# An output projection moved to Strassen's seven products, and two feed-forward prologues given other buffers and four PSUM banks

## The chip, the cores and the metric

The kernel runs on one core of a Trainium2 chip. It is one program; its time is the device time of one execution in microseconds (us). TensorE (PE in the profile) multiplies, VectorE (DVE), ScalarE (ACT) and GpSimd (POOL) work on tiles of 128 partitions, and SyncE (SP) issues the DMAs. Each engine takes its own instructions in order and waits for the others by semaphores.

## The reference, cut to what matters

One layer of a streaming encoder over 1024 tokens of width 1024, in float32:

```
x = x + 1/2 * SwiGLU_1(RMSNorm(x))          # FFN 1, inner width 2816
h = RMSNorm(x); P = h @ W_in
A = sparse attention of parts of P ;  M = mLSTM of other parts of P
x = x + W_out( sigmoid(g_a) * (A @ W_a) + sigmoid(g_b) * (M @ W_b) )
x = x + 1/2 * SwiGLU_2(RMSNorm(x))          # FFN 2
SwiGLU(h) = (silu(h @ w_gate) * (h @ w_up)) @ w_down
```

The change concerns the line with `W_out` (1024 x 1024), and the first step of both FFNs: RMSNorm, the transposes of the normed tokens, and the operands made of them.

## The kernel before, in words

**Precision.** Every float32 operand of a product is split in two: `hi` is a ScalarE copy rounded to the matmul's type, `lo` the VectorE (or GpSimd) difference. `mm3` (L658 to L660) then does three matmuls, hi·hi, hi·lo and lo·hi, of 128x128 by 128x512 each. `split` (L790 on ScalarE, L791 on VectorE) makes such a pair.

**Strassen's form.** The FFN products and the input projection use Winograd's form of Strassen's algorithm: both operands are cut in four blocks, sums and differences of blocks are made, and seven block products (numbered 0 to 6) stand for eight. `Presums` makes the sums of `W_in` once, beside the gate and up products of FFN 1 (`beside`), and stores them in DRAM (`d_s`).

**Prologue of an FFN** (`operands`). Four token tiles are normed (`norm`: Square with a sum on ScalarE L763, the root on VectorE L664 and GpSimd L665, the scaling on VectorE L765) into four buffers `xn` out of the arena `ar`. The squares of `norm` lie in a 1024 column buffer of the same arena. `turned` (L773) transposes 128 columns of four tiles into one of two PSUM banks (`psB`, banks 2 and 3), and `put_turned` evicts it twice on ScalarE (L841, L844) and once on VectorE (L842). After eight of these the four `xn` are freed, and tiles 4 to 7 are normed in place, transposed (evicted by L878) and combined (L879, L880, `put`, `put2`). `gate_up` starts with products 0 and 1 of two column blocks (96 matmuls), which need the first four tiles alone; product 5 needs the others.

**Memory.** `Segment`s are fixed stretches of SBUF in pages of 1024 columns. `ar` and `rr` are arenas over several of them, for plain and for split tiles; they hand out the space that was freed longest ago. `segment(tag, arena)` makes a stretch anew and so waits for its old users. In the first prologue `ar` has 11 pages: 4 `xn`, 4 results of L844, 2 of early weights, and what is left.

**Output projection** (`merge`). For each of eight column blocks c: load the gate (`d_sa`) and the other branch (`d_tb`), take the sigmoid (L2090), multiply `A @ W_a` (24 matmuls, `proj`), on VectorE times the gate and plus the branch (L2095, L2096), and split. After every second block `accumulate` multiplies the two finished blocks with two rows of `W_out` for all eight token tiles (96 matmuls, L805 to L809) and adds each 128x1024 result from PSUM onto the residual `xs` (L810). The rows of `W_out` come through `Weights`, which loads and splits ahead (L185 on ScalarE, L186 on GpSimd). `Pairs` (L240, L251 and L279 to L298) prepares the gate and up weights of FFN 2; its first operands are made before the last `accumulate`.

**Order.** A scheduler writes each engine's order by a simulated timeline, with program order as the priority; so later work can stand before earlier work where its operands come sooner.

`Down` (77 steps of 12 matmuls) is the last product of an FFN; each step splits an activation and a weight tile, loaded six steps ahead (L462).

Of the kernel before, what the change touches and what calls it, by code (L numbers as in the profile page):

```python
# [221 lines left out]
class Pairs:  # L222
# [82 lines left out]
    def prime(self):  # L305
        while self.nl < len(self.loads) and self._load():
            pass
        while self.np < min(len(self.jobs), self.i + self.LOOK) and self._prep():
            pass
# [9 lines left out]
class Presums:  # L319
# [6 lines left out]
    def __init__(self, k, w_in, d_s):  # L326
        self.k, self.w_in, self.d_s = k, w_in, d_s
        self.order = list(dict.fromkeys(i[0] for i in MIXING if i != "ik"))
        self.work = self.steps()

    def steps(self):
        k, nc = self.k, self.k.nc
        for p in self.order:
            two = [None, None]
            while not all(two):
                two = [k.ar.alloc(1024, soft=True) for _ in range(2)]
                if not all(two):
                    for b in two:
                        if b:
                            b.free()  # L340
                    yield
# [21 lines left out]

    def finish(self):
        left = sum(1 for _ in self.work)
        assert not left, left

# [61 lines left out]
class Down:  # L429
# [125 lines left out]
    def run(self, done):  # L555
        k = self.k
        for i, (q, j) in enumerate(self.steps):
            self.prime(i)
# [19 lines left out]
class Block:  # L578
    def __init__(self, tc, pools, a):
        self.tc, self.nc, self.a = tc, tc.nc, a  # L580
        self.sb, self.ps, self.dr = pools
        self.ar, self.rr, self.own = Arena(), Arena(), {}
        self.plain("plain", "more")
        self.round("round", "spare", "extra")
        for t in ("raw", "rawx", "side"):
            self.segment(t, None)
        self.whole_raw = True
        self.w = Weights(self, 0, 0)
        self.bg = ()
        self.due = [0, 0]  # L590

        self.psum = self.ps.tile([P, 4096], F32, name="psum", bufs=1)
        self.turn, self.turnB, self.turnS = 0, 2, 4
        self.last = None
# [26 lines left out]
    def segment(self, tag, arena):  # L621
# [8 lines left out]
        if arena:  # L630
            arena.segs.append(self.own[tag])

# [95 lines left out]
    def plan_weights(self):  # L728
# [8 lines left out]
        def rows(src, r0):  # L737
            v = src[r0:r0 + P, :]
            w.add(src.shape[1], lambda t: dma(t, v))

# [11 lines left out]
        for j in range(8):  # L752
            cols(a["w_proj_a"][0], j * P)
            if j % 2:
                rows(a["w_out"][0], (j - 1) * P)
                rows(a["w_out"][0], j * P)
# [12 lines left out]
    def turned(self, xn, k):  # L769

        ps = self.psB()
# [20 lines left out]


    def accumulate(self, xs, acts, ws, scale, done=None):

        nc = self.nc
        mm = nc.tensor.matmul
        last = len(acts) - 1
        for t in range(8):
            ps = self.psS()  # L800
            for j, (ac, w) in enumerate(zip(acts, ws)):
                ah, al = (b.r[:, t * P:(t + 1) * P] for b in ac)
                wh, wl = w[0].r, w[1].r
                for n in (0, 512):
                    mm(ps[:, n:n + 512], ah, wh[:, n:n + 512], start=j == 0, stop=False)  # L805
                for n in (0, 512):
                    mm(ps[:, n:n + 512], ah, wl[:, n:n + 512], start=False, stop=False)  # L807
                for n in (0, 512):
                    mm(ps[:, n:n + 512], al, wh[:, n:n + 512], start=False, stop=j == last)  # L809
            nc.vector.scalar_tensor_tensor(xs[t].f, ps, scale, xs[t].f, ALU.mult, ALU.add)  # L810
            if done:
                done(t)
        for pair in list(acts) + list(ws):
            for b in pair:
                b.free()
# [30 lines left out]
    def operands(self, xs, gain, spill=None):  # L846
# [6 lines left out]
        for t in range(4):  # L853
            n = ar.alloc(1024)
# [12 lines left out]
        yield 1  # L867
        for t in range(4, 8):
# [152 lines left out]
    def ffn(self, xs, gain, pairs, wd, x_dram, spill=None, first=None, done=None, beside=None):  # L1021
# [24 lines left out]
        down.run(done)  # L1046
# [3 lines left out]
    def late_tokens(self, xs, spill):  # L1050

        nc, v, gain = self.nc, self.nc.vector, self.g_mix
# [1026 lines left out]
    def merge(self, yaT, xs, next_pairs):  # L2079

        nc, ar = self.nc, self.ar
        acts = []
        for c in range(8):
            w = self.w.get()
            hi, lo = (self.either(1024, "side", "extra") for _ in range(2))
            sa, tb, sg = ar.alloc(1024), ar.alloc(1024), self.take("h0", 1024, False)
            nc.sync.dma_start(sa.f, self.d_sa[c])
            nc.sync.dma_start(tb.f, self.d_tb[c])
            with self.tc.issue_after(self.split_A):
                nc.scalar.activation(sg.f, sa.f, AF.Sigmoid)  # L2090
            for th in (1, 0):
                cs = slice(th * 512, th * 512 + 512)
                ps = self.psA(th)
                self.proj(w, yaT, th, ps)
                nc.vector.tensor_tensor(sg.f[:, cs], sg.f[:, cs], ps, ALU.mult)  # L2095
                nc.vector.tensor_tensor(sg.f[:, cs], sg.f[:, cs], tb.f[:, cs], ALU.add)  # L2096
                self.split(hi.r[:, cs], lo.r[:, cs], sg.f[:, cs])
            for b in (*w, sa, tb, sg):
                b.free()
            acts.append((hi, lo))  # L2100
            if c % 2:
                ws = [self.w.get(), self.w.get()]
                if c == 7:
                    self.close("more")
                    next_pairs.prime()
                self.accumulate(xs, acts, ws, 1.0)
                acts = []
        for pair in self.aqT.values():
            for b in pair:
                b.free()  # L2110


    def run(self, x, out):
# [28 lines left out]
        sums = Presums(self, a["w_in"][0], d_s)  # L2142
# [16 lines left out]
        self.ffn(xs, self.g_ffn1, pairs, a["ffn1_w_down"][0], xt, first=self.more_constants, done=half_done, beside=sums.step)  # L2159
# [71 lines left out]
        pairs = Pairs(self, a["ffn2_w_gate"][0], a["ffn2_w_up"][0])  # L2231
        self.merge(yaT, xs, pairs)
        self.segment("side", None)
        self.segment("h0", None)
        self.segment("swap", None)
        self.plain("more")
        self.round("extra")
# [47 lines left out]
```

## Time and profile before

| | us |
|---|---|
| median of 3 runs (2158.54 to 2163.19) | 2161.04 |
| the profiled execution | 2156.2 |
| its span, from the first to the last instruction | 2154.5 |
| TensorE busy in the span | 2067.5 (96%) |
| VectorE busy | 1632.2 (76%) |
| ScalarE busy | 1040.8 (48%) |
| granted TensorE clock, mean of the span | 0.988 |

A busy share is an average over stages with different limits, so the stages below are read one by one from windows of the span. A matmul's row gives its whole passage through the array (some 390 ns); what counts is the distance from one to the next, and that is read from how many fit in a window without a gap.

### The profile page before, as it was taken

Reading aid. Unit: us, or ns where it says so; the run is one execution under the profiler, and the core shown is the slowest. Engines: PE = TensorE matmul, PEld = TensorE weight load, DVE = VectorE, ACT = ScalarE, POOL = GpSimd, SP = SyncE. Lnnn points to the kernel's source line nnn. Section 1 sums busy time; section 2 is a strip of 40 time slices with the busy share of each in tenths; the row PEclk is TensorE's granted clock in tenths of the full one; section 3 lists DMA queues with packets and bytes.
Section 4 is the critical chain, followed back from the end, with each engine's and each line's share of the span. In section 5 each row is a group of like instructions: output and inputs, shape, how many; then the busy total and the mean of one; then the engine's idle time right before and its main releaser. Section 6 shows DMA issues by size and latency. Waiting matters only on the chain.

```text
span 2154.5 us, 27729 instructions
## 1 busy us (share of the span) xinstructions
PE 2067.5 (96%) x9397; PEld 1686.8 (78%) x9397; DVE 1632.2 (76%) x2806; ACT 1040.8 (48%) x1928; POOL 381.2 (18%) x391
## 2 busy tenths in 40 slices
PE   6999999999999999999998999899899999999999
PEld 5788787888887778677777787777688888888887
DVE  6987887678855885988899689665786667669964
ACT  7332233344446664965885578323633333334442
POOL 1000000000303224434445545221000000000300
PEclk9999999999999999999999999999899999999999
DMA  5379994393522324456775222612243333277341
GB/s 181 124 245 291 280 289 153 132 364 125 168 68 92 90 72 120 133 167 178 226 224 164 93 74 70 249 59 88 68 143 108 105 101 113 98 258 276 96 142 40
DMA packets 275466, 326.76 MB, mean 152 GB/s; under 512 B 20236, under 2 KB 185724, under 8 KB 275324
## 3 DMA queue, kind: packets, MB, share of 16 engines
q1 hardware_dynamic: 275324, 324.99, 46.5%
q8 instruction: 74, 1.21, 0.2%
q14 instruction: 68, 0.56, 0.1%
HBM read 224.23 MB, written 100.70 MB: 151 GB/s over the span
## 4 chain that ended last, share of the span: by engine, by line
PE 45%; DVE 10%; ACT 3%; DMA 2%; issue 2%; POOL 0%; SPq 0%; DVEq 0%; ACTq 0%; POOLq 0%
PE psum L658 12%; PE psum L660 12%; PE psum L659 12%; PE psum L1983 1%; DVE plain L1476 1%; PE psum L805 1%; PE psum L809 1%; PE psum L807 1%; DVE h L791 1%; PE psum L1365 1%; PE psum L2038 1%; PE psum L2037 1%; PE psum L1366 1%; ACT plain L1502 0%; ACT round L408 0%
## 5 line engine op out<-in xcount | busy, mean ns | idle before, releaser
L658 PE MATMUL psum<-h,round 128*128 128x512 f32 x656 | 261.8, 400 | 4.2 <-DVE plain L976 1.6
L659 PE MATMUL psum<-h,round 128*128 128x512 f32 x656 | 259.5, 396 | 1.1 <-DVE h L791 0.8
L660 PE MATMUL psum<-h,round 128*128 128x512 f32 x656 | 259.1, 395 | 0.3 <-DVE round L298 0.3
L545 POOL TENSOR_TENSOR swap<-swap,h 128x1024 f32<-128x1024 f32 x12 | 32.9, 2773 | 1014.8 <-DVE h L531 1014.8
L409 POOL TENSOR_TENSOR round<-raw,round 128x512 fp32r<-128x512 f32 x108 | 149.4, 1392 | 155.7 <-ACT round L408 122.1
L658 PEld LDWEIGHTS psum<-h,round 128*128 128x128 f32 x656 | 124.3, 190 | 33.9 <-DVE plain L976 2.0
L660 PEld LDWEIGHTS psum<-h,round 128*128 128x128 f32 x656 | 123.9, 189 | 27.9 <-issue 1.8
L659 PEld LDWEIGHTS psum<-h,round 128*128 128x128 f32 x656 | 124.2, 189 | 26.9 <-DVE h L791 1.3
L658 PE MATMUL psum<-swap,round 128*128 128x512 f32 x328 | 131.6, 406 | 9.9 <-ACT plain L1452 2.6
L660 PE MATMUL psum<-swap,round 128*128 128x512 f32 x328 | 129.9, 397 | 1.2 <-POOL round L409 1.2
L659 PE MATMUL psum<-swap,round 128*128 128x512 f32 x328 | 130.5, 398 | 0.1
L1476 DVE TENSOR_SCALAR_CACHE_REDUCE plain<-plain 128x384 bf16<-128x384 f32 (+1 forms) x124 | 100.3, 808 | 2.5
L297 ACT ACTIVATE round<-plain 128x512 fp32r<-128x512 f32 x75 | 46.8, 630 | 102.4 <-PE psum L659 80.6
L790 ACT ACTIVATE round<-plain 128x512 fp32r<-128x512 f32 x72 | 45.1, 631 | 102.2 <-PE psum L659 90.2
L658 PE MATMUL psum<-h,extra 128*128 128x512 f32 x200 | 80.2, 402 | 6.2 <-ACT h L790 4.9
L658 PEld LDWEIGHTS psum<-swap,round 128*128 128x128 f32 x328 | 63.2, 193 | 27.4 <-ACT plain L1452 3.0
L791 DVE TENSOR_TENSOR round<-plain,round 128x512 fp32r<-128x512 f32 x72 | 55.9, 780 | 37.6 <-ACT round L790 37.3
L408 ACT ACTIVATE round<-raw 128x512 fp32r<-128x512 f32 x108 | 66.4, 622 | 33.4 <-PE psum L659 20.6
L659 PE MATMUL psum<-h,extra 128*128 128x512 f32 x200 | 79.5, 397 | 2.2 <-DVE h L791 2.2
L658 PE MATMUL psum<-h,spare 128*128 128x512 f32 x200 | 78.8, 395 | 1.3 <-DVE plain L976 1.3
L660 PE MATMUL psum<-h,extra 128*128 128x512 f32 x200 | 79.0, 395 | 0.0
L659 PE MATMUL psum<-h,spare 128*128 128x512 f32 x200 | 78.4, 392 | 0.0
(753 smaller groups left out, 5972.5 us busy)
## 6 DMA issues: line engine op xcount, KB each, us to landing
plain<-d_a SPq DMA_DIRECT2D x154, 256.0 KB
d_a<-plain SPq DMA_DIRECT2D x131, 256.0 KB
raw<-in_ffn_w_gate_dram SPq DMA_DIRECT2D x44, 512.0 KB
raw<-d_s SPq DMA_DIRECT2D x74, 256.0 KB
h<-in_ffn_w_down_dram SPq DMA_DIRECT2D x66, 256.0 KB
plain<-in_w_in_dram SPq DMA_DIRECT2D x32, 512.0 KB
d_s<-plain SPq DMA_DIRECT2D x64, 256.0 KB
raw<-in_w_in_dram SPq DMA_DIRECT2D x53, 256.0 KB
```

The costliest lines, as they stand in the source:

```text
L297: k.nc.scalar.activation(hi.r.rearrange("p (k c) -> p k c", k=4), src, AF.Copy)
L408: self.done_A = k.nc.scalar.activation(hi.r, raw.f, AF.Copy).ins
L409: k.nc.gpsimd.tensor_tensor(lo.r, raw.f, hi.f, ALU.subtract)
L545: k.nc.gpsimd.tensor_tensor(x(th, dh), x(th, dh), u, ALU.add)
L658: mm(ps, lhs[0], rhs[0], start=start, stop=False, skip_group_check=more)
L659: mm(ps, lhs[0], rhs[1], start=False, stop=False, skip_group_check=more)
L660: mm(ps, lhs[1], rhs[0], start=False, stop=stop, skip_group_check=more)
L790: self.split_A = self.nc.scalar.activation(hi, src, AF.Copy).ins
L791: self.nc.vector.tensor_tensor(lo, src, hi.bitcast(F32), ALU.subtract)
L805: mm(ps[:, n:n + 512], ah, wh[:, n:n + 512], start=j == 0, stop=False)
L807: mm(ps[:, n:n + 512], ah, wl[:, n:n + 512], start=False, stop=False)
L1476: v.tensor_scalar(s.junk[:, :s.width[j]], s.sc[j], s.cand[:, j:j + 1], None, ALU.is_ge, ALU.add, accum_out=s.cnt[:, j:j + 1])
```

## The change

In `merge`, all eight blocks of the activation y are now made first, in another order (0, 4, 1, 5, ...) and kept unsplit in segment `h0`; `proj` writes to PSUM banks 4 to 7 in turn instead of 0 and 1. Then a new class `Outs` runs seven products of four steps; each step is 12 matmuls over four token tiles and has its own split of y and of a weight block. The sums of y are made on VectorE in `sums`; those of `W_out` are made by `Presums.rows` beside the down product of FFN 1 (every odd step from 35 on) and stored in DRAM (`d_o`). The results are added onto the residual from two groups of four banks. `accumulate` goes.

In `operands`, `xn` comes out of `h0` instead of the arena. While `wide` is set, which is in both FFNs' prologues, `turned` goes round banks 0 to 3. `late_tokens` clears `wide` and calls `level`, which resets the ages by which space is handed out. `Pairs.prime` takes its look-ahead as an argument.

```diff
@@ Presums
+    def rows(self):
+        k, nc = self.k, self.k.nc
+        for j in range(4):
+            two = yield from self.two()
+            for h in range(2):
+                with k.tc.issue_after(k.mark):
+                    nc.sync.dma_start(two[h].f, self.w_out[h * 512 + j * P:h * 512 + j * P + P, :])
+            yield
+            b11, b12, b21, b22 = (b.f[:, c:c + 512] for b in two for c in (0, 512))
+            op = nc.vector.tensor_tensor
+            op(b11, b12, b11, ALU.subtract)
+            op(b12, b22, b12, ALU.subtract)
+            yield
+            op(b22, b22, b11, ALU.subtract)
+            op(b21, b21, b22, ALU.subtract)
+            for q, b in ((4, b11), (6, b12), (5, b22), (3, b21)):
+                nc.sync.dma_start(self.d_o[j, Outs.SLOT[q]], b)
...
+class Outs:
+    ORDER = (0, 5, 1, 4, 2, 6, 3)
+    LOOK = 4
+    LOADS = 6
...
+    def sums(self, j):
+        k, op = self.k, self.k.nc.vector.tensor_tensor
+        (a11, a12), (a21, a22) = ((y[j], y[4 + j]) for y in self.y)
+        s1 = self.s1[j] = k.ar.alloc(512)
+        op(s1.f, a21.f, a22.f, ALU.add)
+        op(a21.f, a11.f, a21.f, ALU.subtract)
+        op(a11.f, s1.f, a11.f, ALU.subtract)
...
+        k.split(ah.r, al.r, a.f)
+        nc.scalar.activation(wh.r, w.f, AF.Copy)
+        (nc.gpsimd if j % 2 else nc.vector).tensor_tensor(wl.r, w.f, wh.f, ALU.subtract)
+        w.free()
+        if q == 1:
+            nc.vector.tensor_tensor(a12.f, a12.f, a11.f, ALU.subtract)
...
@@ Down.run
+            if beside and i > 33 and i % 2:
+                beside()
@@ turned
-        ps = self.psB()
+        if self.wide:
+            self.turnT = (self.turnT + 1) % 4
+            ps = self.bank(self.turnT)
+        else:
+            ps = self.psB()
@@ operands
-            n = ar.alloc(1024)
+            n = self.take("h0", 1024)
...
+        self.segment("h0", None)
         for t in range(4, 8):
             self.norm(xs[t], xs[t])
@@ merge
-        for c in range(8):
+        for n in range(8):
+            c = n // 2 + n % 2 * 4
...
+                ps = self.bank(4 + (2 * n + th) % 4)
                 self.proj(w, yaT, th, ps)
-                nc.vector.tensor_tensor(sg.f[:, cs], sg.f[:, cs], ps, ALU.mult)
-                nc.vector.tensor_tensor(sg.f[:, cs], sg.f[:, cs], tb.f[:, cs], ALU.add)
-                self.split(hi.r[:, cs], lo.r[:, cs], sg.f[:, cs])
+                a = y[th][c].f
+                v.tensor_tensor(a, a, ps, ALU.mult)
+                v.tensor_tensor(a, a, tb.f[:, cs], ALU.add)
+                have.add((th, c))
...
-                self.accumulate(xs, acts, ws, 1.0)
...
+            outs.prime(0, have)
+            if c > 3:
+                outs.sums(c - 4)
...
+        self.segment("swap", None)
+        next_pairs.prime(0)
+        banks = {0: 0, 1: 0, 2: 0, 5: 4, 4: 4, 6: 4, 3: 4}
+        dst = {0: ((0, 1), (1, 0), (1, 1)), 5: ((1, 0),), 1: ((0, 0),), 4: ((1, 1), (0, 1)), 2: ((0, 1),),
+               6: ((1, 1),), 3: ((1, 0),)}
+        for i, (q, j) in enumerate(outs.steps):
+            if i == 21:
+                self.close("more")
+                self.close("side")
+            outs.prime(i)
+            if i > 23:
+                next_pairs.prime(2 * (i - 23))
+            four = outs.ready.pop(i)
+            more = q in (1, 4, 3)
+            for t in range(4):
+                self.mm3(self.bank(banks[q] + t), [b.r[:, t * P:t * P + P] for b in four[:2]],
+                         [b.r for b in four[2:]], j == 0 and not more, j == 3, more)
...
+            if j == 3:
+                for t in (0, 2):
+                    ps = self.bank(banks[q] + t, 2).rearrange("p (t d) -> p t d", t=2)
+                    for th, dh in dst[q]:
+                        x = xv[:, th * 4 + t:th * 4 + t + 2, dh * 512:dh * 512 + 512]
+                        v.tensor_tensor(x, x, ps, ALU.add)
@@ run
+        self.round("side", "extra")
         self.merge(yaT, xs, pairs)
+        self.wide = True
```

More of the change, by code (lines that the diff above doesn't have):

```diff
@@ L333, in steps @@
         for p in self.order:
[L334 to L341, printed above, removed]
+            two = yield from self.two()
             v = [b.f.rearrange("p (k y c) -> p k y c", k=4, y=2) for b in two]
@@ L362, in step, with step_rows, __init__, _load @@
         next(self.work, None)
+    def step_rows(self):
+        next(self.more, None)
     def finish(self):
-        left = sum(1 for _ in self.work)
+        left = sum(1 for w in (self.work, self.more) for _ in w)
         assert not left, left
+class Outs:
+    ORDER = (0, 5, 1, 4, 2, 6, 3)
+    SLOT = {4: 0, 5: 1, 6: 2, 3: 3}
+    LOOK = 4
+    LOADS = 6
+    def __init__(self, k, w_out, d_o, y):
+        self.k, self.w_out, self.d_o, self.y = k, w_out, d_o, y
+        self.steps = [(q, j) for q in self.ORDER for j in range(4)]
+        self.raw, self.ready, self.s1 = {}, {}, {}
+        self.nl = self.np = 0
+    def sums(self, j):
[5 more added lines that the diff above has]
+        op(a11.f, s1.f, a11.f, ALU.subtract)
+    def _load(self):
+        k = self.k
+        q, j = self.steps[self.nl]
+        b = k.ar.alloc(512, soft=True)
+        if b:
+            if q in self.SLOT:
+                src = self.d_o[j, self.SLOT[q]]
+            else:
+                r, c = {0: (0, 0), 1: (512, 0), 2: (512, 512)}[q]
+                src = self.w_out[r + j * P:r + j * P + P, c:c + 512]
+            k.nc.sync.dma_start(b.f, src)
+            self.raw[self.nl] = b
+            self.nl += 1
+        return b
+    def _prep(self, have):
+        k, nc = self.k, self.k.nc
+        q, j = self.steps[self.np]
+        if self.np not in self.raw or not (q == 0 and (0, j) in have or j in self.s1):
+            return False
+        four = [k.rr.alloc(512, soft=True) for _ in range(4)]
+        if not all(four):
+            for b in four:
+                if b:
+                    b.free()
+            return False
+        (a11, a12), (a21, a22) = ((y[j], y[4 + j]) for y in self.y)
+        a = {0: a11, 5: a11, 1: a12, 4: self.s1.get(j), 2: a12, 6: a21, 3: a22}[q]
+        ah, al, wh, wl = four
+        w = self.raw.pop(self.np)
+        k.split(ah.r, al.r, a.f)
[4 more added lines that the diff above has]
+            nc.vector.tensor_tensor(a12.f, a12.f, a11.f, ALU.subtract)
+            a11.free()
+        elif q not in (0, 5):
+            a.free()
+        self.ready[self.np] = four
+        self.np += 1
+        return True
+    def prime(self, i, have=()):
+        while self.nl < min(len(self.steps), i + self.LOADS) and self._load():
+            pass
+        while self.np < min(len(self.steps), i + self.LOOK) and self._prep(have):
+            pass
@@ L631, in segment, with level @@
             arena.segs.append(self.own[tag])
+    def level(self):
+        for s in self.own.values():
+            s.freed = [0] * len(s.freed)
     def close(self, tag):
@@ L752, in plan_weights @@
         for j in range(8):
[L753 to L756, printed above, removed]
+            cols(a["w_proj_a"][0], (j // 2 + j % 2 * 4) * P)
     def norm(self, src, dst):
@@ L791, in split @@
         self.nc.vector.tensor_tensor(lo, src, hi.bitcast(F32), ALU.subtract)
[L794 to L815, printed above, removed]
     def put(self, q, j, src, tag):
@@ L1019, in gate_up, with ffn @@
                 last(q)
-    def ffn(self, xs, gain, pairs, wd, x_dram, spill=None, first=None, done=None, beside=None):
+    def ffn(self, xs, gain, pairs, wd, x_dram, spill=None, first=None, done=None, beside=None, beside_down=None):
         nc, ar, v = self.nc, self.ar, self.nc.vector
@@ L2157, in half_done @@
                 self.late_tokens(xs, spill)
-        self.ffn(xs, self.g_ffn1, pairs, a["ffn1_w_down"][0], xt, first=self.more_constants, done=half_done, beside=sums.step)
+        self.ffn(xs, self.g_ffn1, pairs, a["ffn1_w_down"][0], xt, first=self.more_constants, done=half_done, beside=sums.step,
+                 beside_down=sums.step_rows)
         sums.finish()
```

72 lines of the change are left out of this document (41 added, 31 removed).

## The prediction

> **What bounds the kernel now.** First the page, for the span and which engine fills it. Then a table of windows, one for each stage that the change touches, to turn "96% busy" into time that TensorE really lost. Then TensorE's waits in the two prologues, and last the timeline at the spots that these name.
>
> ```profile
> span 2154.5 us, 27729 instructions
> PE 2067.5 (96%) x9397; PEld 1686.8 (78%) x9397; DVE 1632.2 (76%) x2806; ACT 1040.8 (48%) x1928; POOL 381.2 (18%) x391
> ```
>
> Busy shares and counts in windows; the two rows in the middle are those of the transposes (L773) alone:
>
> ```profile
> 13.40:51.70 38.30, 32.67 (x152) 25.95 (x152) 27.24 (x46) 30.86 (x55) 3.56 (x4) 0.94 0.46 150
> 51.70:80.00 28.30, 27.73 (x107) 21.31 (x108) 26.87 (x35) 14.44 (x21) 0.00 (x0) 0.90 0.22 66
> 1354.80:1491.60 136.80, 134.51 (x582) 109.25 (x582) 88.19 (x101) 36.46 (x55) 23.71 (x15) 0.99 0.36 132
> 1491.60:1536.20 44.60, 35.10 (x154) 26.64 (x154) 23.48 (x40) 30.53 (x51) 4.11 (x5) 0.88 0.20 70
> 1536.20:1560.00 23.80, 21.56 (x79) 16.99 (x80) 23.80 (x30) 11.26 (x15) 0.00 (x0) 0.80 0.12 36
> 1560.00:1600.00 40.00, 39.95 (x176) 32.48 (x175) 36.07 (x60) 13.50 (x23) 0.00 (x0) 1.00 0.48 159
> ...
> 13.40:51.70 38.30, 9.54 (x56) 7.69 (x56) 0.94 0.46 150
> 1491.60:1536.20 44.60, 10.99 (x58) 7.63 (x58) 0.88 0.20 70
> ```
>
> The last stage row (1560 to 1600) is TensorE at its best: 176 matmuls in 40.00 us, 0.2273 us each, at clock 1.00. With that as the yardstick the other rows tell what was lost. A transpose is shorter; its price is in the timeline of TensorE, where four of them occupy 0.35 us, 0.09 each:
>
> ```profile
> 1518.75 0.60 PE L773 MATMUL psum<-ident,plain 128*128 128x128 f32 x4
> 1519.10 0.48 PE L660 MATMUL psum<-swap,spare 128*128 128x512 f32 x1
> ```
>
> - The output projection (1354.8 to 1491.6): 582 rows, of them 576 matmuls, 130.9 us, and 6 transposes, 0.5. Of 136.8 us 5.4 are lost. It is bound by the number of matmuls.
> - The prologue of FFN 2 (1491.6 to 1560, 68.4 us): 233 rows, 58 of them transposes (5.2 us), 175 matmuls (39.8). Lost: 23.4 us.
> - The prologue of FFN 1 (13.4 to 80, 66.6 us): 259 rows, 56 transposes (5.0), 203 matmuls (46.1). Lost: 15.5 us. What lies ahead of 13.4 waits for the first loads, and nothing in the change reaches it.
>
> What TensorE waits for in them, FFN 2 first, then FFN 1:
>
> ```profile
> PE psum L773 <- DVE plain L664: 4.3, 2, 2.9
> PE psum L658 <- ACT h L790: 2.9, 1, 2.9
> PE psum L659 <- DVE h L791: 2.2, 1, 2.2
> ...
> PE psum L773 <- ACT side L878: 3.3, 4, 2.4
> PE psum L658 <- ACT h L790: 2.2, 2, 2.0
> ```
>
> These add up to half of what was lost. The rest is the clock that goes down after an idle stretch: the two FFN 2 rows above have 0.88 and 0.80. At the first gap one sees it matmul by matmul:
>
> ```profile
> 1494.48 0.65 PE L773 MATMUL psum<-ident,plain 128*128 128x128 f32 x2 [2.89 <-DVE plain L664]
> 1495.69 0.80 PE L658 MATMUL psum<-swap,round 128*128 128x512 f32 x1 [0.56 <-ACT swap L841]
> ...
> 1500.97 0.59 PE L658 MATMUL psum<-swap,round 128*128 128x512 f32 x1
> 1501.40 0.40 PE L659 MATMUL psum<-swap,round 128*128 128x512 f32 x1
> ```
>
> Thirteen matmuls in 5.7 us, 0.2 too long each: a gap of some 3 us costs near 3 more.
>
> Why the second half of a prologue comes late is in ScalarE's timeline, FFN 2 and FFN 1:
>
> ```profile
> 1519.06 1.06 ACT L763 ACTIVATE plain<-h 128x1024 f32<-128x1024 f32 x1 [4.04 <-PE psum L773]
> ...
> 32.67 1.06 ACT L763 ACTIVATE plain<-h 128x1024 f32<-128x1024 f32 x1 [0.81 <-PE psum L773]
> ```
>
> Those are the squares of tiles 4 and later. They need nothing from a transpose; they wait for room. Four `xn`, four results and two of early weights leave one of 11 pages, so the square writes where `xn` lay, and `xn` is free after the last of the 32 transposes (1518.75 above). The residual, though, was complete one eviction after 1491.6, the end of the projection's window: some 26 us of ScalarE and VectorE time were left half used (VectorE has 23.48 of 44.60), and then VectorE is full (23.80 of 23.80).
>
> **The change, part by part.**
>
> *Matmuls of the output projection.* The activation keeps 8 x 24 = 192. `accumulate` had 4 x 96 = 384; seven products of four steps of twelve are 336. 48 go: 48 x 0.2273 = 10.9 us, all on TensorE's path.
>
> *Its waits.* Of the 5.4 lost, 1.4 are the clock at the start (0.99 in the row), which stays. Each `accumulate` stood behind a fresh activation's multiply, add and split; with the activation first, four of these are ready when the products begin, and the next are made four steps (10.9 us) ahead. New are the boundaries: product 3 uses the banks of product 6, right behind it. Here are VectorE's rows in this stage, and one spot where GpSimd works beside it:
>
> ```profile
> L810 DVE SCALAR_TENSOR_TENSOR h<-psum,h 128x1024 f32<-128x1024 f32 x31 | 37.5, 1222 | 26.6 <-PE psum L809 26.5
> L2096 DVE TENSOR_TENSOR h<-h,plain 128x512 f32<-128x512 f32 x16 | 14.4, 900 | 0.6
> L2095 DVE TENSOR_TENSOR h<-h,psum 128x512 f32<-128x512 f32 x16 | 11.0, 687 | 12.2 <-PE psum L660 11.7 <-ACT h L2090 0.5
> ...
> 1468.24 2.41 POOL L186 TENSOR_TENSOR more<-raw,more 128x1024 fp32r<-128x1024 f32 x1 [26.63 <-ACT more L185]
> 1469.54 1.67 DVE L298 TENSOR_TENSOR spare<-raw,spare 128x512 fp32r<-128x512 f32 x1
> ```
>
> The first two banks of product 6 are done 12 of its last 24 matmuls ahead of the rest, so one eviction of 1.22 us is exposed at most, there and a little at the others. I keep 3 of the 5.4 and count 2.4 as gained; bounds 0 and 4.
>
> *Does VectorE keep up?* The 28 steps are 336 x 0.2273 = 76.4 us. VectorE has 24 splits of y (four lie in the first phase), 12 differences of weights, 4 sums, 40 x 0.69 = 27.6; 20 evictions (3+1+1+2+1+1+1, twice) x 1.22 = 24.4, where before there were 32; 4 splits for FFN 2, 2.8; and from the prologue 4 scalings and 8 L842 at 0.75, 9.0. Together 63.8 of 76.4. GpSimd takes the other 14 differences, 1.2 us each by the L186 row (2.41 for twice the width), 16.9, in place of 15 instructions and 23.7 us now. What that does to VectorE: L2096 has the shape of L2095 and both inputs in SBUF, and takes 900 instead of 687 ns; 16 x 0.21 = 3.4 us for 23.7 of GpSimd, so 2.4 here. That leaves 10 us of room, and I count nothing.
> The Trainium skill's page "SBUF — State Buffer" (Terms, shared port pair) says that VectorE and GpSimd share a port pair as an exclusive lock, and that the loser waits for the whole instruction. By it all 16.9 would be VectorE's, 80.7 in all, more than the 76.4. The L298 row, 1.67 beside the 2.41 of GpSimd, agrees for one instruction; the mean of 900 does not for all.
>
> *First phase and DMA.* 192 matmuls in 43.6 us want gate and branch tiles that were spread over 130. Rows of SyncE and of the DMA:
>
> ```profile
> 1358.18 3.77 SPq L2230 DMA_DIRECT2D h<-d_x  x8
> 1386.38 0.32 SPq L2088 DMA_DIRECT2D plain<-d_tb  x1
> ...
> 1360.00:1380.00 20.00, 20.00 (x90) 16.53 (x90) 14.38 (x18) 6.30 (x8) 2.40 (x1) 1.00 0.95 372
> ```
>
> Already now the last of them is issued at 1386.4, behind the residual's eight loads at 1358. Six `W_out` blocks ahead add 1.6 MB, 4 us at 372 GB/s: 1391. The last column block begins at 1354.8 + 168 x 0.2273 = 1393, and its four PSUM banks hide 10.9 us more. So 0; bound +5, should the nine pages of `plain` hold them back.
>
> *Prologue of FFN 2.* Products 6 and 3 touch only tokens 4 to 7, so tokens 0 to 3 are final 96 matmuls, 21.8 us, before the end, and banks 0 to 3 are free then. Prices of ScalarE:
>
> ```profile
> L878 ACT ACTIVATE side<-psum,par 128x512 f32<-128x512 f32 x8 | 5.5, 693 | 0.1
> L763 ACT ACTIVATE plain<-h 128x1024 f32<-128x1024 f32 x4 | 4.2, 1051 | 4.2 <-PE psum L773 4.0
> L297 ACT ACTIVATE extra<-plain 128x512 fp32r<-128x512 f32 x4 | 2.5, 638 | 1.7 <-DVE plain L287 1.7
> L967 ACT ACTIVATE plain<-psum 128x512 f32<-128x512 f32 x4 | 2.2, 606 | 0.7 <-PE psum L660 0.7
> ```
>
> In these 21.8 us ScalarE has 5 steps of two copies and 4 for FFN 2 (14 x 0.63 = 8.8), 4 squares (4.2) and 16 evictions like L878 (11.1): 24.1. So some 3 us slip past the end, but of the later four columns only: product 0 starts at once, behind the last eviction, 1.2 us. Its cover for the second half is the same 96 matmuls, 21.8 us. ScalarE needs there 3 + 4.2 + 5.5 + 12 weight and operand copies (7.6) + 4 L967 and 2 more (3.6), 24; besides, the spill of tokens 4 to 7 must leave before the norm overwrites them. I take 2 us late, and 5 more for order and clock. Of 23.4 lost 8.2 stay: gain 15.2. Bounds: 6 (the first gap and its cold clock alone) and 22.
>
> *Prologue of FFN 1.* Same two edits, without the early half. Up to product 5 (51.7) ScalarE is busy 30.86 of 38.3: 7.4 us is the most that order can win ahead of it. I take 5; bounds 0 and 7.4.
>
> *Sums of W_out beside the down product, and the middle.* Totals of 552 to 668, and of 700 to 1340:
>
> ```profile
> sum 116.00, PE 116.00 PEld 95.99 DVE 78.34 ACT 55.45 POOL 21.23; mean PE 38.67 PEld 32.00 DVE 26.11 ACT 18.48 POOL 7.08
> ...
> sum 640.00, PE 602.36 PEld 488.80 DVE 532.56 ACT 450.13 POOL 277.60; mean PE 301.18 PEld 244.40 DVE 266.28 ACT 225.07 POOL 138.80
> ```
>
> 16 subtractions are 11 us of VectorE where 37.7 are free, and 24 DMAs share SyncE's queue with the loads of `Down`, which are six steps (16 us) ahead: 0, bound +2.7, one step. In the middle no work changes, but `level` hands out space in another order; TensorE is not busy for 37.6 of 640 us there, and I let a tenth of that go either way: 0, bounds -4 and +4.
>
> **Sum.** -10.9 - 2.4 - 15.2 - 5 = -33.5 us. Against the profiled execution (2156.2, 1.7 above its span) that is 2122.7; the median shown is 4.8 higher, so I forecast 2161.0 - 33.5 = 2127.5, say 2128.
>
> **The rivals.**
> - *The prologues stay full.* ScalarE (30.53 of 44.60) or VectorE (23.80 of 23.80) sets their length, or the scheduler still writes the first norms behind the last product. Then 13.3 for the projection and 6 for the first gap of FFN 2: 2142. For it speaks VectorE without idle time from 1536 to 1560; against it its 21 idle us in the window before.
> - *All the lost time goes:* 14.9 + 22 + 7.4, 2117; with a kind middle 2113.
> - *Slower: VectorE paces the products.* If GpSimd blocks it in full (80.7 against 76.4), it has no room, and each eviction is exposed where its banks are used again: 7.3 us for product 0, 2.4 for 5, 2.4 for 1, 4.9 for 4, 2.4 for 6, 19.4 in all, with 4.3 for the pace and some three cold clocks of 2.8, 32. The early half then is late too and FFN 2 gains nothing: -13.3 - 5 + 32, 2175. It decides from 18 us of exposed waits on. Against it: the 900 ns, and that an eviction reads one input from PSUM; L810 keeps its 1222 beside GpSimd. The page on SBUF is behind this one.
>
> **How the numbers follow.** Forecast (2120 to 2136) 0.56, full prologues (2136 to 2152) 0.26, all gone (under 2120) 0.10, slower 0.05, and 0.03 that several bounds add up to no change. The range 2112 to 2152 takes in the first three. 0.2% is 4.3 us, about what a measurement here can tell: faster 0.92, same 0.03, slower 0.05.
>
> **What would show it.** In the changed kernel: a projection of 123 to 125 us from its first matmul to its last, with 528 matmuls; no row of TensorE waiting for an eviction over 2 us at a product's start; squares of the first four tiles some 20 us before the end of product 3, those of the others within 5 us after it; no gap near 3 us, and a clock over 0.95, at the seam. The forecast is wrong if VectorE shows no idle time in the products, or if product 5 of either FFN still stands behind L790 or L878.

## The result and the profile after

The changed kernel takes **2124.2 us** (median of 4 runs, 2121.01 to 2126.59), the one before 2160.48 (2158.54 to 2163.19): a ratio of 0.983, 95% interval 0.9813 to 0.9848, 36 us less. The forecast was 2128. The total was right; several terms of its sum were not.

First the page of the changed kernel, then windows of it (columns as in the prediction: length; busy time of PE, PEld, DVE, ACT, POOL with counts; clock; DMA share; GB/s). The third row is the seam that was at 0.88 and 0.80:

```profile
span 2121.7 us, 27881 instructions
PE 2046.8 (96%) x9349; PEld 1675.9 (79%) x9349; DVE 1650.1 (78%) x2852; ACT 1055.6 (50%) x1968; POOL 383.5 (18%) x397
```

```profile
1362.20:1404.00 41.80, 40.88 (x169) 33.20 (x170) 31.84 (x51) 15.92 (x29) 4.44 (x4) 0.93 0.85 313
1404.00:1482.00 78.00, 78.00 (x355) 64.81 (x354) 63.25 (x85) 38.81 (x68) 19.12 (x14) 1.00 0.26 88
1482.00:1524.00 42.00, 41.71 (x207) 34.59 (x206) 40.57 (x59) 34.70 (x56) 3.23 (x4) 1.00 0.33 120
13.40:51.70 38.30, 34.85 (x165) 27.22 (x165) 34.47 (x55) 35.66 (x60) 2.95 (x4) 1.00 0.46 151
51.70:80.00 28.30, 27.20 (x119) 21.53 (x118) 27.03 (x40) 11.44 (x17) 0.00 (x0) 1.00 0.33 112
```

In the products TensorE is busy 78.00 of 78.00 us and VectorE 63.25; the seam has 41.71 of 42.00. The complete list of TensorE's waits from the projection to the end of the prologue (1362 to 1560):

```profile
PE psum L769 <- ACT swap L898: 1.4, 1, 1.4
PE psum L770 <- DVE swap L899: 0.9, 1, 0.9
PE psum L771 <- DVE round L298: 0.3, 1, 0.3
```

No eviction is among them. And the last square of the first four tiles, then the first and the last of the other four, on ScalarE:

```profile
1461.42 1.05 ACT L867 ACTIVATE plain<-h 128x1024 f32<-128x1024 f32 x1
...
1482.80 1.04 ACT L867 ACTIVATE plain<-h 128x1024 f32<-128x1024 f32 x1
...
1487.63 1.06 ACT L867 ACTIVATE plain<-h 128x1024 f32<-128x1024 f32 x1
```

**Where the time went.** Seven events that both kernels have cut the program into seven stages. Their rows in the timeline, before and then after: the first eviction of product 5 in FFN 1, the last eviction of product 5 there, the last eviction of `Down`, the last row of the attention's softmax, the last eviction of the output projection, the first eviction of product 5 in FFN 2, the last eviction of its `Down`:

```profile
70.39 1.28 DVE L976 TENSOR_TENSOR plain<-plain,psum 128x512 f32<-128x512 f32 x2
437.54 0.69 DVE L976 TENSOR_TENSOR plain<-plain,psum 128x512 f32<-128x512 f32 x1 [1.36 <-PE psum L660]
670.70 2.60 DVE L531 SCALAR_TENSOR_TENSOR swap<-psum,swap 128x1024 f32<-128x1024 f32 x2 [2.85 <-PE psum L660]
1345.30 0.19 ACT L1972 ACTIVATION_READ_ACCUMULATOR plain<-plain,h 128x1 f32 x1
1491.62 1.23 DVE L810 SCALAR_TENSOR_TENSOR h<-psum,h 128x1024 f32<-128x1024 f32 x1
1557.24 1.29 DVE L976 TENSOR_TENSOR plain<-plain,psum 128x512 f32<-128x512 f32 x2
2148.16 2.58 DVE L531 SCALAR_TENSOR_TENSOR swap<-psum,swap 128x1024 f32<-128x1024 f32 x2 [13.23 <-PE psum L660]
```

```profile
63.32 0.68 DVE L1061 TENSOR_TENSOR plain<-plain,psum 128x512 f32<-128x512 f32 x1
433.06 0.69 DVE L1061 TENSOR_TENSOR plain<-plain,psum 128x512 f32<-128x512 f32 x1 [1.36 <-PE psum L771]
672.08 1.23 DVE L634 SCALAR_TENSOR_TENSOR swap<-psum,swap 128x1024 f32<-128x1024 f32 x1 [0.16 <-PE psum L771]
1351.72 0.20 ACT L2059 ACTIVATION_READ_ACCUMULATOR plain<-plain,h 128x1 f32 x1
1480.84 2.34 DVE L2225 TENSOR_TENSOR h<-h,psum 128x1024 f32<-128x1024 f32 x2
1523.43 0.68 DVE L1061 TENSOR_TENSOR plain<-plain,psum 128x512 f32<-128x512 f32 x1
2115.33 2.58 DVE L634 SCALAR_TENSOR_TENSOR swap<-psum,swap 128x1024 f32<-128x1024 f32 x2 [13.23 <-PE psum L771]
```

The two first evictions of product 5 count by their start, the others by start plus duration. The stages of the profiled runs, in us:

| stage | before | after | difference | forecast |
|---|---|---|---|---|
| prologue of FFN 1 | 70.4 | 63.3 | -7.1 | -5 |
| its gate and up products | 367.8 | 370.4 | +2.6 | 0 |
| its down product | 235.1 | 239.6 | +4.5 | 0, bound +2.7 |
| the middle, to the attention's last softmax | 672.2 | 678.6 | +6.4 | 0, bounds ±4 |
| output projection | 147.4 | 131.3 | -16.1 | -13.3 |
| prologue of FFN 2 | 64.4 | 40.3 | -24.1 | -15.2 |
| the rest | 593.5 | 594.5 | +1.0 | 0 |
| sum | 2150.7 | 2117.9 | -32.8 | -33.5 |

The sum is of one profiled run each. That of the kernel before lies 4.3 us below its median, that of the changed kernel 0.8 below; so the stages add up to 32.8, where the medians are 36 apart.

In this table the three stages that were to gain won 13.8 more than forecast, and the stages counted at nothing lost 14.5. But 3.2 us on each side are only the border. In the changed kernel 14 of the projection's 528 matmuls run ahead of the last softmax, twelve of them well inside the attention, where the kernel before has none; the first is, on TensorE:

```profile
1322.72 0.39 PE L771 MATMUL psum<-swap,round 128*128 128x512 f32 x1
```

Counted with the projection (14 at 0.2273 us each), they leave -12.9 there and +3.2 in the middle: 10.6 won beyond the forecast, and 11.3 lost. The experiments ask which edit won the prologue, and what was lost. In the tables below the middle of every kernel with the seven products holds 12 to 14 such matmuls, some 3 us. (Some expectations below count stages between starts of rows, which gives figures up to 2 us other than these tables.)

### The profile page after: what moved, and what is told of

The parts are those of the page before. It is cut to its first block, busy times and chain, and to the rows that moved or that the text cites. A ratio compares the mean times of both kernels' runs of the same rounds, so it can differ in the third digit from the quotient of the medians.

```text
span 2121.7 us, 27881 instructions
## 1 busy us (share of the span) xinstructions
PE 2046.8 (96%) x9349; PEld 1675.9 (79%) x9349; DVE 1650.1 (78%) x2852; ACT 1055.6 (50%) x1968; POOL 383.5 (18%) x397
## 5 line engine op out<-in xcount | busy, mean ns | idle before, releaser
L648 POOL TENSOR_TENSOR swap<-swap,h 128x1024 f32<-128x1024 f32 x12 | 32.8, 2771 | 1020.5 <-DVE h L634 1020.5
L769 PE MATMUL psum<-swap,round 128*128 128x512 f32 x312 | 125.8, 404 | 11.2 <-DVE plain L1237 6.9
L770 PE MATMUL psum<-swap,round 128*128 128x512 f32 x312 | 124.1, 398 | 1.1 <-DVE swap L899 0.9
L771 PE MATMUL psum<-swap,round 128*128 128x512 f32 x312 | 123.8, 397 | 0.2 <-POOL round L512 0.2
L769 PE MATMUL psum<-h,extra 128*128 128x512 f32 x200 | 78.3, 392 | 2.2 <-DVE plain L1205 1.6
L769 PE MATMUL psum<-side 128*128 128x512 f32 x204 | 79.4, 389 | 0.0
L770 PE MATMUL psum<-side 128*128 128x512 f32 x204 | 79.4, 389 | 0.0
```

The source lines that it names most:

```text
L648: k.nc.gpsimd.tensor_tensor(x(th, dh), x(th, dh), u, ALU.add)
L769: mm(ps, lhs[0], rhs[0], start=start, stop=False, skip_group_check=more)
L770: mm(ps, lhs[0], rhs[1], start=False, stop=False, skip_group_check=more)
L771: mm(ps, lhs[1], rhs[0], start=False, stop=stop, skip_group_check=more)
```

## Experiments: which edit won the prologue

Four kernels. `prologues_only` is the kernel before with the edits of `operands`, `turned` and `level`:

```diff
-            n = ar.alloc(1024)
+            n = self.take("h0", 1024)
...
-        ps = self.psB()
+        if self.wide:
+            self.turnT = (self.turnT + 1) % 4
+            ps = self.bank(self.turnT)
```

> The kernel before, with its own output projection, and only the prologues' edits: xn out of h0, transposes round four banks, and the levelled ages. Theory (the prologues gain on their own, because the squares of tiles 4 to 7 no longer wait for the 32nd transpose): FFN 2's prologue loses about 10 less, the first gap (2.9 us and its cold clock) stays because the residual is still complete only one eviction after the last matmul; FFN 1's prologue gains 7 that are half given back by the down product: 2160 - 10 - 3 = 2147. Rival (ScalarE and VectorE are full in the prologues, so order wins nothing; the whole gain was the projection's and its early half's): 2156 to 2160.

`proj_only` is the changed kernel with those two edits taken back, `xn_arena` with the first of them taken back:

> The changed kernel with xn out of the arena and the transposes in two banks again: the seven products and the early half alone. Theory: the projection's 17 us stay, of FFN 2's prologue the first gap goes (6) and the second half still waits for the 32nd transpose, 10 of the 23 lost again; the attention's longer tail (5) stays: 2160 - 17 - 13 + 5 + 2 = 2137, that is 13 above the changed kernel. Rival 1 (the prologue's edits do nothing, all is the projection): 2124 to 2127. Rival 2 (without the buffers the early half cannot start): 2148.

> The changed kernel with xn out of the arena again, transposes in four banks. Theory (xn in h0 is what frees the squares of tiles 4 to 7): second halves of both prologues wait for the 32nd transpose again; FFN 2 loses about 6, FFN 1's 7 come back but the down product had given them away already, so 0 to 2: 2131. Rival (the four banks are what counts, or after the early half there is room in the arena): 2124.

`two_last` takes the early half away and leaves the buffers:

```diff
-    ORDER = (0, 5, 1, 4, 2, 6, 3)
+    ORDER = (0, 5, 1, 4, 6, 3, 2)
```

> The changed kernel with the products in the order 0, 5, 1, 4, 6, 3, 2: the last product now ends on tokens 0 to 3, so the norms of the first four tiles cannot begin ahead of the end, while the others are final 48 matmuls earlier. Everything else as in the changed kernel. Theory (the early half is what removes the first gap and gives the second half its cover): the first gap of FFN 2 comes back with its norms, four squares, transposes and evictions, 6 to 12 us: 2124 + 9 = 2133. Rival (buffers and banks alone won the 23 us): 2124 to 2126.

Measured, with the stages of their profiled runs:

| kernel | median, us | ratio to before (95%) | prologue 1 | middle | projection | prologue 2 |
|---|---|---|---|---|---|---|
| before | 2161.21 | 1 | 70.4 | 672.2 | 147.4 | 64.4 |
| prologues_only | 2135.22 | 0.9879 (0.9866 to 0.9892) | 62.8 | 670.8 | 149.6 | 42.9 |
| proj_only | 2152.05 | 0.9966 (0.9952 to 0.998) | 72.3 | 679.5 | 131.8 | 61.7 |
| xn_arena | 2136.49 | 0.9887 (0.9875 to 0.99) | 68.8 | 683.4 | 132.2 | 49.2 |
| two_last | 2144.24 | 0.9919 (0.9906 to 0.9932) | 63.5 | 682.0 | 131.0 | 55.9 |
| after | 2124.2 | 0.983 (0.9813 to 0.9848) | 63.3 | 678.6 | 131.3 | 40.3 |

The prologues' edits alone are worth 26 us, twice what I expected; the seven products alone 9, less than expected. `prologues_only` takes 21.5 us off the prologue of FFN 2 with the old projection, to whose order I had given no early half. Its squares, on ScalarE, tell why it has one (third, fourth, fifth and eighth of eight):

```profile
1476.25 1.06 ACT L769 ACTIVATE plain<-h 128x1024 f32<-128x1024 f32 x1 [2.01 <-DVE h L820]
1478.75 1.06 ACT L769 ACTIVATE plain<-h 128x1024 f32<-128x1024 f32 x1 [1.35 <-DVE h L820]
1481.56 1.06 ACT L769 ACTIVATE plain<-h 128x1024 f32<-128x1024 f32 x1 [1.66 <-DVE h L820]
...
1495.85 1.05 ACT L769 ACTIVATE plain<-h 128x1024 f32<-128x1024 f32 x1
```

`accumulate` goes through the token tiles in order, one eviction (here L820) every 2.5 to 4.4 us, and the third to the sixth square begin as soon as their tile's has ended. So the old projection had an early half as well. In the kernel before it served three tiles only, as the third and the fourth square on ScalarE, the fourth tile's last eviction on VectorE and the last matmuls of the projection on TensorE show:

```profile
1478.96 1.06 ACT L763 ACTIVATE plain<-h 128x1024 f32<-128x1024 f32 x1 [2.02 <-DVE h L810]
1480.21 1.21 DVE L810 SCALAR_TENSOR_TENSOR h<-psum,h 128x1024 f32<-128x1024 f32 x1
1490.97 0.61 PE L809 MATMUL psum<-more,side 128*128 128x512 f32 x2
1491.67 1.06 ACT L763 ACTIVATE more<-h 128x1024 f32<-128x1024 f32 x1 [0.94 <-issue]
```

The third tile's square comes right behind its eviction; the fourth's comes 10.2 us after its eviction has ended. It writes to `more`, which the projection's last matmuls read until 1491.58; it starts 0.09 us later. `turned` takes columns of all four tiles, so the first gap of the prologue comes of this missing buffer. With `xn` elsewhere the arena has room, and the delay is gone.

Both edits count: from `proj_only` to `xn_arena` four banks bring 12.5 us of prologue 2, and from there to the changed kernel `xn` in `h0` brings 8.9. Buffers are needed and not enough, as `two_last` shows: its last product ends on tokens 0 to 3, and its first square and first transposes are these, on ScalarE and TensorE:

```profile
1489.81 1.06 ACT L867 ACTIVATE plain<-h 128x1024 f32<-128x1024 f32 x1 [0.84 <-DVE round L298]
...
1495.51 3.14 PE L881 MATMUL psum<-ident,h 128*128 128x128 f32 x12 [4.78 <-DVE plain L775]
```

TensorE stands still for 4.78 us. Of the 20 us more, 15.6 are in this prologue: the rival falls, and the price is above the 6 to 12 that I expected.

## Experiments: what the other stages lost

**ScalarE at the attention's end.** In the changed kernel, on ScalarE and TensorE:

```profile
1355.66 0.63 ACT L452 ACTIVATE side<-plain 128x512 fp32r<-128x512 f32 x1 [1.62 <-DMA plain<-in_w_out_dram]
...
1359.68 0.47 PE L2124 MATMUL psum<-more,extra 128*128 128x512 f32 x1 [2.97 <-DVE h L2084]
```

A copy for the products stands in ScalarE's queue ahead of the attention's last steps and waits for its load. `w_after_y` holds these copies back:

```diff
-        nc.scalar.activation(wh.r, w.f, AF.Copy)
+        with k.tc.issue_after(k.split_A): nc.scalar.activation(wh.r, w.f, AF.Copy)
```

> The changed kernel with one edit: ScalarE's copy of a W_out block (L452) may not stand ahead of the split before it in the program, so that it can't be put into the attention's last steps, where in the changed kernel it waited 1.62 us for its load and four copies of the attention queued behind it. Theory (this queueing is why the attention's tail is 4 to 5 us longer than before, with TensorE idle 2.97 us there and at 0.83 of its clock): 2124 - 4.5 = 2119.5. Rival (the tail is longer because of the DMA, 0.98 busy with six more blocks, and the copies only stand where ScalarE waits anyway): 2123 to 2125, the 2.97 us wait still there.

2126.84 us (0.9847, 0.9832 to 0.9861), middle 678.9: nothing won. Its rows, on ScalarE and TensorE:

```profile
1360.29 0.63 ACT L185 ACTIVATE side<-raw 128x512 fp32r<-128x512 f32 x1 [2.17 <-DMA raw<-in_w_proj_a_dram]
...
1363.08 0.47 PE L2124 MATMUL psum<-more,extra 128*128 128x512 f32 x1 [2.27 <-DVE h L2084]
```

The next weight copy in the queue (L185, which the kernel before has too) takes the place of the first, and waits 2.17 us for its own load. Only the queue's head was replaced, and the late loads remained; what a head without any wait would bring was not tested. And there was little to win, for the kernel before has such a wait at the same place:

```profile
1349.32 0.47 PE L2037 MATMUL psum<-round,extra 128*128 128x512 f32 x1 [2.80 <-DVE h L1997]
```

From the last softmax to the unbroken run of the projection's matmuls the kernel before takes 9.3 us, and the changed kernel 10.3, in which ten of the projection's matmuls (2.3 us) are done. So from there on the tail was not 4 to 5 us longer.

**VectorE beside GpSimd.** In the down product TensorE waits where W_out's sums (L352) are made, in the changed kernel:

```profile
554.79 8.42 POOL L648 TENSOR_TENSOR swap<-swap,h 128x1024 f32<-128x1024 f32 x3
555.31 2.89 DVE L352 TENSOR_TENSOR plain<-plain 128x512 f32<-128x512 f32 x1
558.12 5.64 DVE L899 TENSOR_TENSOR round<-plain,round 128x512 fp32r<-128x512 f32 x2
...
563.82 0.50 PE L770 MATMUL psum<-round 128*128 128x512 f32 x1 [2.73 <-DVE round L899]
```

L648 adds product 5 of `Down` onto the residual, six times back to back on GpSimd, 16.4 us in all, from 546.8 on. Beside it one VectorE subtraction takes 2.8 to 2.9 us instead of 0.69: one passes for each GpSimd instruction. The old kernel had this stretch too, without the additional subtraction, and TensorE has no wait there. Four kernels change one side, or both:

```diff
rows_pool:  -            op = nc.vector.tensor_tensor        # in Presums.rows
            +            op = nc.gpsimd.tensor_tensor
rows_late:  -            if beside and i > 33 and i % 2:
            +            if beside and i > 48 and i % 2:
swap_dve:   -                    k.nc.gpsimd.tensor_tensor(x(th, dh), x(th, dh), u, ALU.add)   # L648
            +                    v.tensor_tensor(x(th, dh), x(th, dh), u, ALU.add)
late_swap:  the edits of rows_late and swap_dve
```

> The changed kernel with the 16 subtractions of W_out's blocks beside FFN 1's down product on GpSimd in place of VectorE; the order on TensorE and ScalarE is the same. Theory (VectorE, full in 560 to 570, makes TensorE wait 2.73 and 1.08 us there): both waits go, 2124 - 3.8 = 2120. Rival 1 (the rows are hidden and the waits come from Down's own splits, whose buffers or loads come late): 2124. Rival 2 (GpSimd holds VectorE up for as long as its subtraction lasts): no gain or 1 to 2 us slower.

> The changed kernel with W_out's sums begun at step 50 of the down product in place of 35, so clear of the evictions of the products in between. Theory (too much for VectorE in that one stretch): the waits at 563.8 and 592.4 go and none as large comes later, 2124 - 3 = 2121. Rival (a step's subtractions are exposed wherever they stand, or the store of the sums keeps the loads of Down back): 2124 or above.

> The changed kernel with the six additions of Down's product 5 (L648, 128x1024, in each FFN) on VectorE in place of GpSimd. In the changed kernel GpSimd does them back to back for 14 us, and in this stretch each VectorE subtraction takes 2.88 us in place of 0.68. Theory (VectorE can pass only one instruction for each of GpSimd's; W_out's subtraction L352 in that stretch cost 2.89 and not 0.69, and that made TensorE wait): six VectorE additions of 1.2 us cost 7, and five or six subtractions get 2.2 shorter each, 12; the waits of TensorE at 563.8 and 592.4 go, 2124 - 3.5 = 2120.5. In the second FFN no wait of TensorE hangs on it: 0. Rival (the subtractions are slow for another reason, their operands come late from the DMA at 0.5 share): they stay at 2.88, VectorE has 7 us more, 2126 to 2130.

> The changed kernel with both edits: W_out's sums from step 50 on, and L648 on VectorE. Theory (each takes the same stall away, one by moving the subtractions out of GpSimd's stretch, the other by taking GpSimd out): no more than one alone, 2120 to 2123. Rival (two different costs): 2117.

| kernel | median, us | ratio to before (95%) | gate and up 1 | down 1 | middle |
|---|---|---|---|---|---|
| after | 2124.2 | 0.983 (0.9813 to 0.9848) | 370.4 | 239.6 | 678.6 |
| rows_pool | 2127.64 | 0.9852 (0.9838 to 0.9865) | 374.8 | 239.6 | 680.8 |
| rows_late | 2123.65 | 0.9831 (0.9818 to 0.9845) | 372.4 | 235.1 | 678.0 |
| swap_dve | 2125.0 | 0.9843 (0.9831 to 0.9856) | 371.7 | 235.1 | 682.1 |
| late_swap | 2126.07 | 0.9849 (0.9834 to 0.9864) | 374.6 | 235.1 | 679.1 |

The mechanism is shown, in `swap_dve` by VectorE's rows:

```profile
550.34 0.69 DVE L352 TENSOR_TENSOR plain<-plain 128x512 f32<-128x512 f32 x1
550.95 3.50 DVE L648 TENSOR_TENSOR swap<-swap,h 128x1024 f32<-128x1024 f32 x3
554.35 0.69 DVE L899 TENSOR_TENSOR round<-plain,round 128x512 fp32r<-128x512 f32 x1
```

The same additions take 1.2 us each on VectorE, the subtractions are back at 0.69, no wait of TensorE is left there, and the down product takes 235.1 us, as before. Moving the sums away (`rows_late`) gives the same 235.1, and both together no more. The subtractions on GpSimd only make its work there longer (239.6). But the 4.5 us show in none of the medians: in the profiled runs other stages took them back. With such differences one has to be careful. `two_last` and the changed kernel have the same order on every engine up to the projection's products, and yet differ by 5.3 us in the gate and up products and 3.4 in the middle; TensorE's waits from 64 to 434 are 5.8 us in the changed kernel and 8.9 in `two_last`.

**The products beside GpSimd.** `all_pool` puts all 28 differences of W_out's blocks on GpSimd:

```diff
-        (nc.gpsimd if j % 2 else nc.vector).tensor_tensor(wl.r, w.f, wh.f, ALU.subtract)
+        nc.gpsimd.tensor_tensor(wl.r, w.f, wh.f, ALU.subtract)
```

> The changed kernel with all 28 differences of W_out's blocks on GpSimd in place of 14. GpSimd then works some 28 x 1.3 = 36 of the products' 76 us; VectorE has 14 (of which 12 in the products) x 0.69 = 8 us less. Theory (beside GpSimd a VectorE operation with both inputs in SBUF takes some 0.2 us longer, not as long as GpSimd's): the same time within 2 us, 2122 to 2126, TensorE without waits for evictions. Rival (by the Trainium skill's page on SBUF VectorE waits for GpSimd's whole instruction): VectorE 63 - 8 + 18 or more, without idle time, and waits at the products' ends: 2130 or more.

2126.44 us (0.9848, 0.9834 to 0.9863): the time of the changed kernel within the intervals, as the theory had it, but not for its reason. The evictions from PSUM (L2225) and the subtractions of y (L457) as groups of VectorE in the products (count, then busy us and mean ns), first of the changed kernel, then of `all_pool`, and the window of `all_pool`:

```profile
L2225 DVE TENSOR_TENSOR h<-h,psum 128x1024 f32<-128x1024 f32 x20 | 23.6, 1215 | 2.9 <-PE psum L771 2.5
...
L457 DVE TENSOR_TENSOR h<-h 128x512 f32<-128x512 f32 x4 | 2.7, 682 | 0.0
```

```profile
L2225 DVE TENSOR_TENSOR h<-h,psum 128x1024 f32<-128x1024 f32 x20 | 23.5, 1213 | 3.2 <-PE psum L771 2.9
...
L457 DVE TENSOR_TENSOR h<-h 128x512 f32<-128x512 f32 x4 | 4.6, 1179 | 0.0
```

```profile
1404.00:1482.00 78.00, 78.00 (x355) 64.84 (x354) 64.23 (x77) 38.70 (x68) 32.41 (x25) 1.00 0.27 88
```

With both inputs in SBUF the mean goes from 682 to 1179 ns; the evictions, with one input in PSUM, stay at 1213. GpSimd works 13 us more than in the changed kernel (32.41 against 19.12), VectorE has eight instructions fewer, and its busy time is 1 us higher (64.23 against 63.25): what it was relieved of, it lost in waiting.

**The price of the sums.** `rows_only` is `prologues_only` with W_out's loads, subtractions and stores beside the down product, as in the changed kernel. Its projection is the old one and doesn't read them. The code is that of `rows` and `Down.run` in the diff.

> The kernel with the prologues' edits alone (2135) and, beside FFN 1's down product, the loads, subtractions and stores of W_out's sums as in the changed kernel; its projection is the old one and doesn't read them. Theory for the down product: 4 to 5 us more there than in the kernel with the prologues' edits alone (239 in place of 234.6 from the last gate and up corner to the last of Down's evictions): 2139 to 2140. For the stretch from there to the attention's end, 672 in that kernel and 679 to 684 in all with the seven products: theory A (the sums and their DMAs disturb the start of the middle): 677 or more, 2144; theory B (the projection's own early work and its other order of weights do it): 672.

2147.44 us (0.9944, 0.9929 to 0.9959) against the 2135.22 of `prologues_only`: **the sums alone cost 12 us**. Of its profiled run's stages gate and up have 0.9 more, the down product 240.3 against 235.1, the middle 677.3 against 670.8. In the down product it is again one subtraction in GpSimd's stretch, on VectorE, and TensorE behind it:

```profile
560.34 2.88 DVE L352 TENSOR_TENSOR plain<-plain 128x512 f32<-128x512 f32 x1
...
568.82 0.50 PE L702 MATMUL psum<-round 128*128 128x512 f32 x1 [2.87 <-DVE round L838]
```

For the middle theory A held in that the sums lengthen it, without any work of the new projection. The order that the scheduler writes for ScalarE is the same in both kernels up to the start of the middle and another one from there, and beside it stand longer waits of TensorE for VectorE. From 665 to 800, of `rows_only` and then of `prologues_only`, which has no counterpart to the second line:

```profile
PE psum L820 <- DVE swap L808: 3.0, 3, 1.1
PE psum L1416 <- DVE round L1382: 1.9, 1, 1.9
```

```profile
PE psum L783 <- DVE swap L771: 1.2, 2, 0.7
```

For the middle it does not decide where the sums stand, as the last kernel shows. `rows_gate` makes them beside the gate and up products:

```diff
     def step(self):
         next(self.work, None)
+        self.ns = getattr(self, "ns", 0) + 1
+        if self.ns % 4 == 0:
+            next(self.more, None)
```

> The changed kernel with W_out's sums made beside FFN 1's gate and up products (every fourth of the calls that make W_in's sums) in place of beside its down product. Theory (16 subtractions at 0.69 us and 1.2 + 4 MB of DMA cost nothing where no GpSimd work stands beside VectorE, and the middle keeps the order it has without them): down 234.6 in place of 239.0, from there to the attention's end 672 to 676 in place of 679.6, gate and up the same 367 to 374: 2124 - 4.4 - 4 = 2116, between 2113 and 2120. Rival 1 (the gate and up products, where VectorE is busy 246 of 320 us and the DMA 0.73, pay for them): 2120 to 2126, the gate and up stretch longer than 374. Rival 2 (the middle keeps its 679 to 682, since its order hangs on more than the sums): 2120 to 2122.

2120.74 us (2118.34 to 2121.59; 0.9821, 0.9808 to 0.9835): the lowest median of all, in an interval that overlaps that of the changed kernel. Gate and up 369.5, down 235.1, as the theory said; the middle keeps 680.6, as rival 2 said. All twelve kernels with W_out's sums, the changed one among them, have 677 to 683 in the middle, 675 to 681 with the projection's matmuls taken out; the two without the sums have 671 and 672. Another order alone hardly explains it. In the middle ScalarE's instructions stand in nearly the same sequence in `rows_gate` as in `prologues_only` (97 of 100 agree; between `rows_only` and `prologues_only` it is 66), and yet `rows_gate` has 677.4 there, without the projection's matmuls, against 670.8. Nor is it `level`, which `prologues_only` has too. A single run can't price it to better than some 4 us: `proj_only` and `xn_arena` have one and the same sequence on ScalarE and VectorE in the middle, and 679.5 and 683.4. Whether it is where buffers lie, what the 24 DMAs do to later ones, or chance in part, stays open.

## Why the prediction was right, step by step

- **Fewer matmuls and their waits.** -13.3 was forecast; with the 14 early matmuls counted in, -12.9 came. 10.9 are the 48 matmuls. By the prediction's yardstick (0.2273 us a matmul, 0.09 a transpose) TensorE lost 13.1 us in this stage before and 9.6 after, 3.5 less where 2.4 were counted; 1.5 go to the transposes of the next prologue, which now stand here. The 3 us kept for exposed evictions at the products' boundaries were not needed: the list above has none. One sign did not come: 123 to 125 us from the first matmul to the last, since the first twelve run early (1322.72), inside the attention.
- **VectorE in the products.** 63.8 us were counted, 63.25 measured; the 20 evictions take 23.6 (24.4 counted). The slower rival, VectorE pacing the products, did not come: TensorE has 78.00 of 78.00. But the step behind it was wrong. I took the mean of 900 ns against 687 as a mild surcharge. The Trainium skill's page "SBUF — State Buffer" (SBUF: two separate sides) says that a VectorE instruction with two SBUF inputs and a GpSimd instruction that reads SBUF exclude each other for a whole instruction; the 2.89 us beside L648, back at 0.69 when L648 moves, agree with it. What made my reading of it too dark, 80.7 us, was to add up all of GpSimd's time: only subtractions and additions that meet it wait, and evictions from PSUM don't.
- **Prologue of FFN 2.** -15.2 forecast with a bound of 22, -24.1 measured. By the yardstick 22.1 us were lost in this stage before and 1.3 after, so 20.8 are lost time won; the other 3.3 are work outside the borders, 24 transposes that now run during the projection and 5 matmuls. That the squares of tiles 4 to 7 wait for room was right, and so was what to look for: the first squares end 20 us ahead, the others begin within 5 us of product 3's end. The step that failed is the 8.2 us that I let stay for lateness, order and clock, of which 1.3 stayed. And the early half was put down to the seven products' order; `prologues_only` shows that the old order had one, which lacked room and banks.
- **Prologue of FFN 1.** -5 forecast, -7.1 at its end, within the bounds. That this would reach the end was assumed, not argued: in the eleven kernels with the quick prologue of `prologues_only` and of the change, the gate and up products take 369.5 to 375.7 instead of 367.8.
- **W_out's sums "beside" the down product: 0, bound +2.7.** The step that failed. VectorE's 37.7 free us in the stage were an average; in the 14 us that counted it was full with blocked subtractions. All in all `rows_only` puts 12 us on the sums. In `proj_only` the gate and up products, the down product and the middle (368.4, 237.1 and 679.5) lose 9.9 us of the 15.6 that its projection wins.
- **The middle: ±4.** +6.4 by the table, outside the bounds; +3.2 without the projection's matmuls, inside them. But the reason given, the ages reset by `level`, was not it: `prologues_only` has that edit and 670.8.

So the mechanisms of the gains were right, but the total came out right by luck: gains undersized by 10.6 us met costs of 11.3 that were set at nothing.

## What to carry to other kernels

Before work is put beside a stage for free, look at the shortest stretch in which the engine is full and at what runs beside it on GpSimd, since idle time over the whole stage says nothing about that stretch. When a prologue starts late, look first for the buffer or bank that its first instruction writes, and only then at the order of the producer: here room and banks won 21.5 us without touching the producer. And count a product's preparation with it: seven products instead of eight saved 13 us where they run, and the sums for their operands cost 12 in a kernel that had nothing else of them.

## What the hardware did that was not expected

Beside back-to-back GpSimd additions of 2.8 us, VectorE subtractions with both inputs in SBUF take 2.88 us instead of 0.69, one for each GpSimd instruction. VectorE evictions with an input in PSUM keep their 1.2 us beside GpSimd. The addition that takes GpSimd 2.8 us takes VectorE 1.2.
